# First loads in quarter rows, first products one channel tile at a time, masks first, and longer clock warm-up, in a one-core hybrid decoder block

## The chip, the cores and the metric

The kernel runs on one core of a Trainium2 chip. The metric is the device time of one execution in microseconds (us), from runs without a profiler; the profile is one more execution, taken with the hardware profiler. TensorE is called PE here, VectorE DVE, ScalarE ACT, GpSimd POOL, and SyncE (which issues all the loads) SP.

## What is computed

One layer of a decoder with two groups of heads side by side, for 512 tokens (four tiles of 128) and 1024 channels (eight channel tiles of 128):

```python
h = _rms_norm(x, norm_w[l])
proj = jnp.einsum("btd,dc->btc", h, w_in[l])          # 1024 -> 4096 columns
hq, hf, hi, hg, aq, ak, av, ag = jnp.split(proj, split_points, axis=-1)
o_h = _rms_norm(_hgrn2(hq, hf, hi, lower_bounds[l]), hg_norm_w[l]) * silu(hg)
o_a = _moba(aq, ak, av, q_norm_w[l], k_norm_w[l]) * silu(ag)
x = x + jnp.einsum("btc,cd->btd", concat([o_h, o_a]), w_out[l])
```

Only the start of the first line pair matters here: the transposed, weighted x and its product with the first 512 columns of w_in (`hi`). The row factor of the RMS norm is applied later, when products leave PSUM.

## The kernel before

All is float32. To multiply at near float32 precision, each operand is split into a high part (rounded to the fast matmul format) and a low part (the remainder), and each product is three matmuls: high by high, low by high, high by low. One of these, 128 rows by 512 columns, is called a product below.

**Loads.** SP issues everything in the order of the string `DSEQ`: `x00` is half 0 (512 channels) of token tile 0, 256 KB; `w0` is a weight tile, 256 rows by 512 columns, 512 KB, that is two channel tiles; `nw` is the norm weight, `v` the small vectors. A weight tile lands in `raw`; `split_hi` (ACT, line 109) casts it to `whi`, `split_lo` (DVE, line 117; for weight tile 3 POOL) makes `wlo`.

**Start of PE.** The string `SEQ` is the order by hand of everything up to the end of the first group of columns. Its words, with the functions they call:

- `y7`: `warm_up`, 7 matmuls of 128 by 128 on a tile of ones, whose result nobody reads. The profile has two records for each.
- `nt`: `nw_col`, the norm weight turned into a column (`nwc`).
- `t` a kp: `x_turn`, four transposes: token tiles 2a and 2a+1, channel tiles 2kp and 2kp+1; ACT then copies them out as `hTh` in two instructions 256 wide (line 258). `l` a kp: `x_lo`, DVE makes `hTl` in two instructions (line 266).
- `wh`, `wl` n: the split of weight tile n.
- `p` u kp: `part_hi`, four products of token tile u with weight tile kp (high x with high w, low x with high w, for two channel tiles); `q` u kp: `part_lo`, two products with the low weights.
- `sq` i: ACT squares and sums token tile i; `rs`: the RMS factors (DVE, then POOL); `cv`, `rr`, `cm`: constants, the row of factors, and memory clearing.

The four token tiles' sums stay in four PSUM tiles (`accs`). So before the first product PE transposes all four token tiles for channel tiles 0 to 3 (`t00 t01 t10 t11`, 16 transposes), and then works `p00 q00 p10 q10 p30 q30 p20 q20 ...`. After this string come `p` and `q` of weight tile 3, then seven more groups of columns, the two mixers and the output projection, in an order that a small planner (`drive`) writes down at build time from estimated latencies. The constant masks (`const_tri`) are written at the start of that, in `fill_a`, and the scheduler puts their DVE instructions wherever DVE has room.

Each load has one of eight semaphores in turn, so that the ninth load waits on SP until the first has landed.

Of the kernel before, what the change touches and what calls it, by code (L numbers as in the profile page):

```python
# [8 lines left out]
F32 = mybir.dt.float32  # L9
F32R = mybir.dt.float32r  # L10
I32 = mybir.dt.int32
AF = mybir.ActivationFunctionType
ALU = mybir.AluOpType
# [8 lines left out]
def kernel(  # L22
# [12 lines left out]
    nc = tc.nc  # L35
    P = 128
# [9 lines left out]
    xv = x[0].rearrange("(i p) c -> p i c", p=P)  # L46
# [3 lines left out]
    big = ctx.enter_context(tc.tile_pool(name="big", bufs=1))  # L50
    wpool = ctx.enter_context(tc.tile_pool(name="wpool", bufs=WB))
# [3 lines left out]
    ptr = ctx.enter_context(tc.tile_pool(name="ptr", bufs=2, space=bass.MemoryType.PSUM))  # L55
# [6 lines left out]
    xt = []  # L62
# [5 lines left out]
    def load_x(i, halves=(0, 1)):  # L68
        for hf in halves:
            cs = slice(hf * 512, hf * 512 + 512)  # L70
            nc.sync.dma_start(out=xt[i][:, cs], in_=xv[:, i, cs])  # L71

    def load_vec():
        nc.sync.dma_start(out=vec[0:4, :], in_=lb_logits.rearrange("o (h d) -> (o h) d", d=P))
        nc.sync.dma_start(out=vec[4:5, :], in_=hg_norm_w)
        for r in range(2):
            nc.sync.dma_start(out=vec[5:6, r * DH:(r + 1) * DH], in_=q_norm_w)
            nc.sync.dma_start(out=vec[6:7, r * DH:(r + 1) * DH], in_=k_norm_w)
# [3 lines left out]
    stream = [(w_in[0], c0, kp) for c0 in order for kp in range(KT // 2)]  # L82
# [3 lines left out]
    W = {}  # L86
    raws = {}
    raw0 = []

    def load(n):  # L90
# [11 lines left out]
            in_=src[kp * 256:(kp + 1) * 256, c0:c0 + 512].rearrange("(k p) c -> p k c", p=P))  # L102
        raws[n] = raw

    def split_hi(n):
        raw = raws.pop(n)
        hi = wpool.tile([P, 2, 512], F32R, tag="whi", name="whi")
        lo = wpool.tile([P, 2, 512], F32R, tag="wlo", name="wlo")
        nc.scalar.copy(hi, raw)  # L109
        W[n] = (hi, lo)  # L110
        W["raw", n] = raw
# [13 lines left out]

    POOL_LO = (3,)
    LAT = dict(lm=4.544, lev0=9.2567, lev=4.4882, copy=1.9908, rms=5.7036, silu=15.1764, qk=14.2881, soft=2.5598, softn=0.0041, acopy=4.5215, st=1.5748, ch=6.6909, DEPTH=2)
    SEQ = 'y7 nt t00 wh0 t01 sq0 t10 l00 t11 wl0 p00 q00 l01 wh1 p10 q10 l10 p30 q30 wl1 t03 l11 p20 q20 t12 t02 sq1 p01 q01 wh2 l03 l12 sq3 wh3 p21 q21 p11 q11 sq2 l02 p31 q31 wl2 p32 q32 rs wl3 p02 q02 p22 q22 cv t13 p12 q12 rr cm l13'
    DSEQ = 'x00 nw x10 w0 x20 x30 x01 x31 x11 w1 x21 w2 w4 v w3 w5'
    POOL_LO = (3,)  # L130
    for w in DSEQ.split():
        if w == "nw":
            nc.sync.dma_start(out=vec[32:40, :], in_=norm_w.rearrange("o (k p) -> (o k) p", p=P))  # L133
        elif w == "v":
            load_vec()
        elif w[0] == "x":
            load_x(int(w[1]), (int(w[2]),))
        else:
            load(int(w[1]))
    for n in range(WB, WB + RB):  # L140
# [31 lines left out]
    def mm(o, a, b, start, stop, us):  # L172
        nc.tensor.matmul(o, a, b, start=start, stop=stop)  # L173
        clock[0] += us

    def tr(o, a):
        nc.tensor.transpose(o, a, ident)  # L177
        clock[0] += 0.109
# [82 lines left out]
    def x_lo(a, kp):  # L261
        tp = X["tp", a, kp]
        for d in range(2):
            kt = 2 * kp + d
            ts_ = slice(a * 256, a * 256 + 256)
            nc.vector.scalar_tensor_tensor(hTl[:, kt, ts_], tp[:, d * 256:d * 256 + 256], nwc[:, kt:kt + 1],
                                           hTh[:, kt, ts_].bitcast(F32), op0=ALU.mult, op1=ALU.subtract)


    def acc_tile(wide):  # L270
        return (psc if wide else pacc).tile([P, 512], F32, tag="sc" if wide else "acc", name="acc")
# [465 lines left out]
    def const_tri():  # L737
        prow = const.tile([P, 1], I32, name="prow")
        nc.gpsimd.iota(prow, pattern=[[0, 1]], base=0, channel_multiplier=1)
        ccol = const.tile([P, 32], I32, name="ccol")  # L740
        nc.gpsimd.iota(ccol, pattern=[[1, 32]], base=0, channel_multiplier=0)
        s32 = const.tile([P, 1], I32, name="s32")
        nc.vector.tensor_single_scalar(s32, prow, 31, op=ALU.bitwise_and)
        sb = s32.to_broadcast([P, 32])
        xr = const.tile([P, 32], I32, name="xr")
        nc.vector.tensor_tensor(xr, ccol, sb, op=ALU.bitwise_xor)
        gt = const.tile([P, 32], I32, name="gt")
        nc.vector.tensor_tensor(gt, ccol, sb, op=ALU.is_gt)
        dd = const.tile([P, 32], I32, name="dd")
        nc.vector.tensor_tensor(dd, xr, gt, op=ALU.mult)  # L750
        nc.vector.tensor_single_scalar(eqf, xr, 0, op=ALU.is_equal)
        nc.vector.tensor_single_scalar(lmask[:, 0, :], dd, 1, op=ALU.is_ge)
        for n, l in enumerate((2, 4)):
            bit = 1 << (l - 1)
            nc.vector.tensor_single_scalar(lmask[:, 3 * n + 1, :], dd, bit, op=ALU.is_ge)
            sbit = const.tile([P, 1], I32, name=f"sbit{l}")
            nc.vector.tensor_single_scalar(sbit, prow, bit, op=ALU.bitwise_and)
            for z in range(2):
                side = const.tile([P, 1], I32, name=f"side{l}{z}")
                nc.vector.tensor_single_scalar(side, sbit, z * bit, op=ALU.is_equal)  # L760
                part = const.tile([P, 32], I32, name=f"part{l}{z}")
                nc.vector.tensor_tensor(part, dd, side.to_broadcast([P, 32]), op=ALU.mult)
                nc.vector.tensor_single_scalar(lmask[:, 3 * n + 2 + z, :], part, 2 * bit, op=ALU.is_ge)
# [35 lines left out]


    def fill_a():
        const_tri()
        yield from group(1, True, ev_f)
        yield from group(2, True, ev_silu_t(q2[:, 0]))
        yield from group(3, False, ev_silu(G))
        yield from group(4, True, ev_silu_t(gT))
        const_dist()
        yield from group(5, False, ev_qk("K", ("f", "k", "i", "KL"), kgs))
        yield from group(6, False, ev_qk("Q", ("q",), qgs))
        yield from group(7, False, ev_v)  # L810

    with tc.manual_schedule(engines={mybir.EngineType.PE}):
        with tc.manual_schedule():
            accs = {}

            def part(u, kp, low):
                us = slice(u * P, (u + 1) * P)
                if u not in accs:
                    accs[u] = acc_tile(u >= 2)
                hi, lo = W[kp]  # L820
                for d in range(2):
                    kt = 2 * kp + d
                    wh, wl = hi[:, d, :], lo[:, d, :]
                    prods = ((hTh[:, kt, us], wl),) if low else ((hTh[:, kt, us], wh), (hTl[:, kt, us], wh))
                    for j, (a, b) in enumerate(prods):
                        mm(accs[u], a, b, kt == 0 and not low and j == 0, kt == KT - 1 and low, 0.216)

            def part_hi(u, kp):
                part(u, kp, False)

            def part_lo(u, kp):
                part(u, kp, True)

            acts = dict(cm=const_masks, cv=const_vec, sq=x_sq, rs=x_rstd, rr=x_rows, y=warm_up, nt=nw_col, t=x_turn, l=x_lo, p=part_hi, q=part_lo,
                        wh=split_hi, wl=split_lo)
            for w in SEQ.split():
                name = w.rstrip("0123456789")
                acts[name](*([int(w[1:])] if name == "y" else [int(ch) for ch in w[len(name):]]))
            for n in range(4, WB):
                split(n)  # L840
            for u in range(4):
                part_hi(u, 3)
                part_lo(u, 3)
                ev_i(u, accs[u])
            for kp in range(4):
                del W[kp]
                split(kp + WB)

        q2 = big.tile([P, 2, HH, T], F32, tag="q", name="q2")
        q = q2[:, 1]  # L850
        G = big.tile([P, NT, 512], F32, tag="G", name="G")
        gT = big.tile([P, NP, T], F32, tag="gT", name="gT")
        spawn(levels(0))
        spawn(levels(1))
        spawn(states())
        spawn(chunks())
        fa = fill_a()
        started = [False]

        def filler():  # L860
            yield from fa
            start_attention()
            wait_for(*[("read", n) for n in range(NT)])
            yield from out_h()

        drive(filler())
        for _ in out_a():
            pass
# [27 lines left out]
```

## Time and profile before

| | us |
|---|---|
| median of 3 runs (lowest, highest) | 295.99 (295.94, 296.63) |
| the profiled execution | 297.17 |
| its span, first to last instruction | 295.4 |
| PE busy in the span | 287.6 (97%) |
| DVE, ACT, POOL busy | 175.0, 132.7, 57.1 |

The profiled execution took 1.18 us more than the median of the runs. PE is busy nearly throughout; the exception that concerns the change is the first 11 us. A matmul's record covers more than its share of the pipeline, so what a matmul costs is read from the distance between the starts of two that follow each other.

### The profile page before, as it was taken

What the parts mean: (1) busy time and instruction counts of PE and PEld (TensorE: products, weight loads), DVE (VectorE), ACT (ScalarE), POOL (GpSimd) and SP (SyncE); (2) the same over time, 40 slices, a digit from 0 to 9 for tenths busy, and PEclk for the clock granted to TensorE, in tenths of its full rate; (3) what the DMA queues carried; (4) which work ended last, traced back from release to release, by engine and by line L of the source; (5) the groups of instructions that cost most, each with busy time, mean ns of one, the idle gap of its engine ahead of it and who ended that gap; (6) DMA issues with size and microseconds to landing.
All of it is one profiled execution on the core that took longest, in us unless ns stands there. A gap on an engine that the chain in (4) does not pass through costs nothing.

```text
span 295.4 us, 5115 instructions
## 1 busy us (share of the span) xinstructions
PE 287.6 (97%) x1945; PEld 236.7 (80%) x1945; DVE 175.0 (59%) x379; ACT 132.7 (45%) x248; POOL 57.1 (19%) x92
## 2 busy tenths in 40 slices
PE   7799999999999999999999999999999999999995
PEld 6588888888787777898888888888887787878884
DVE  3552653653699998357855785585384585653232
ACT  3754644420430475225511743753577676763000
POOL 1004201064000000010274223320004534330000
PEclk9999999999999999999999999999999999999999
DMA  6972375160260006100620099468287000000123
GB/s 189 352 282 104 15 106 201 43 242 0 73 213 4 2 2 227 60 0 0 215 73 0 8 261 208 95 168 207 47 229 279 0 2 0 2 2 2 71 101 112
DMA packets 21546, 31.00 MB, mean 105 GB/s; under 512 B 1413, under 2 KB 8338, under 8 KB 21522
## 3 DMA queue, kind: packets, MB, share of 16 engines
q1 hardware_dynamic: 21522, 30.68, 35.5%
q8 instruction: 15, 0.25, 0.3%
q14 instruction: 9, 0.07, 0.1%
HBM read 25.17 MB, written 2.10 MB: 92 GB/s over the span
## 4 chain that ended last, share of the span: by engine, by line
PE 93%; DMA 5%; SPq 1%; DVE 0%; issue 0%; DVEq 0%
PE acc L173 74%; PE tp L177 6%; PE ot L173 4%; PE sc L173 3%; PE pl L173 3%; DMA res<-in_x_dram 3%; DMA x<-in_x_dram 2%; PE ops L173 2%; PE us L173 1%; SPq L71 0%; DVE res L681 0%; SPq L100 0%; DVE res L717 0%; SPq L133 0%; PE tpv L778 0%
## 5 line engine op out<-in xcount | busy, mean ns | idle before, releaser
L173 PE MATMUL acc<-whi,hTh 128*128 128x512 f32 x160 | 65.3, 408 | 0.0
L173 PE MATMUL acc<-whi,hTl 128*128 128x512 f32 x160 | 63.0, 394 | 0.0
L173 PE MATMUL acc<-wlo,hTh 128*128 128x512 f32 x160 | 60.0, 391 | 0.0
L117 DVE TENSOR_TENSOR wlo<-raw,whi 128x1024 fp32r<-128x1024 f32 x39 | 47.1, 1230 | 12.1 <-ACT whi L109 11.6
L109 ACT CAST whi<-raw 128x1024 fp32r<-128x1024 f32 x40 | 41.5, 1048 | 13.4 <-DMA raw<-in_w_in_dram 6.3
L173 PE MATMUL acc<-hTh,whi 128*128 128x512 f32 x96 | 38.2, 397 | 0.0
L173 PE MATMUL acc<-hTh,wlo 128*128 128x512 f32 x96 | 37.5, 391 | 0.0
L173 PE MATMUL acc<-hTl,whi 128*128 128x512 f32 x96 | 37.4, 389 | 0.0
L163 POOL TENSOR_TENSOR r<-v,mh 128x8 f32<-128x8 f32 (+1 forms) x12 | 17.2, 1430 | 99.6 <-DVE v L161 99.5
L173 PEld LDWEIGHTS acc<-whi,hTl 128*128 128x128 f32 x160 | 30.3, 190 | 6.4
L173 PEld LDWEIGHTS acc<-whi,hTh 128*128 128x128 f32 x160 | 30.3, 190 | 6.3
L173 PEld LDWEIGHTS acc<-wlo,hTh 128*128 128x128 f32 x160 | 30.4, 190 | 5.9
L615 POOL TENSOR_SCALAR scr<-scr,rl 128x512 f32<-128x512 f32 (+3 forms) x32 | 17.0, 536 | 47.2 <-DVE rl L614 38.5
L173 PEld LDWEIGHTS acc<-hTh,wlo 128*128 128x128 f32 x96 | 18.0, 188 | 4.0 <-DVE wlo L117 0.2
L173 PEld LDWEIGHTS acc<-hTh,whi 128*128 128x128 f32 x96 | 18.0, 188 | 3.6
L173 PEld LDWEIGHTS acc<-hTl,whi 128*128 128x128 f32 x96 | 18.1, 188 | 3.5
L612 ACT ACTIVATE scr<-scr,nm 128x512 f32<-128x512 f32 (+3 forms) x32 | 17.7, 556 | 6.7 <-DVE nm L608 6.4
L173 PE MATMUL acc<-whi,mTa 128*128 128x512 f32 (+1 forms) x72 | 20.4, 367 | 0.0
L681 DVE TENSOR_TENSOR res<-acc,res 128x512 f32<-128x512 f32 x15 | 10.3, 689 | 15.7 <-PE acc L173 13.3
L177 PE MATMUL tp<-ident,scr 128*128 128x128 f32 x128 | 19.1, 275 | 0.0
L608 DVE CUSTOM_DVE_ANT_0 scr<-sc,bias 128x512 f32<-128x512 f32 (+3 forms) x32 | 14.6, 487 | 6.5 <-PE sc L173 6.2
L177 PEld LDWEIGHTS tp<-ident,scr 128*128 128x128 f32 x128 | 15.0, 140 | 4.0 <-issue 1.4
(138 smaller groups left out, 428.4 us busy)
## 6 DMA issues: line engine op xcount, KB each, us to landing
raw<-in_w_in_dram SPq DMA_DIRECT2D x32, 512.0 KB, 3.7
raw<-in_w_out_dram SPq DMA_DIRECT2D x8, 512.0 KB, 3.9
x<-in_x_dram SPq DMA_DIRECT2D x8, 256.0 KB, 6.4
res<-in_x_dram SPq DMA_DIRECT2D x2, 1024.0 KB, 9.1
out_dram<-res SPq DMA_DIRECT2D x7, 256.0 KB, 2.0
K<-K SPq DMA_DIRECT2D x8, 128.0 KB, 5.9
KL<-KL SPq DMA_DIRECT2D x8, 128.0 KB, 5.9
Q<-scr SPq DMA_DIRECT2D x8, 128.0 KB, 3.7
```

The source lines that it names most:

```text
L109: nc.scalar.copy(hi, raw)
L117: eng.tensor_sub(lo, raw, hi.bitcast(F32))
L163: nc.gpsimd.tensor_tensor(r, v, mh[:, 0:n], op=ALU.pow)
L173: nc.tensor.matmul(o, a, b, start=start, stop=stop)
L177: nc.tensor.transpose(o, a, ident)
L608: nc.vector.tensor_tensor_reduce(out=z[:, 0:n], in0=sc[:, 0:n], in1=bias[:, j, T - n:T], op0=ALU.add, op1=ALU.min, scale=1.0, scalar=3e38, ...
L612: nc.scalar.activation(z[:, 0:n], z[:, 0:n], AF.Exp, bias=nm, scale=-1.0, accum_out=l)
L615: nc.gpsimd.tensor_scalar(z[:, 0:n], z[:, 0:n], rl, 1.0, op0=ALU.mult, op1=ALU.mult)
L681: nc.vector.tensor_tensor(res[hf][:, u, :], ps, res[hf][:, u, :], op=ALU.add)
```

## The change

The new words are: `X` i qr, a quarter row (256 channels, 128 KB) of token tile i; `W` d, 128 rows (256 KB) of weight tile 0; `ct`, the masks, now first; `s` i kp, two transposes for one token tile (`x_turn1`), with copies 128 wide; `k` i kp, the low part of the same; `A0`, `B0`, the high part of the two halves of weight tile 0 (ACT); `a0`, `b0`, their low parts (DVE); `H` u kt and `L` u kt, the two high products and the one low product of token tile u with a single channel tile.

```diff
-    SEQ = 'y7 nt t00 wh0 t01 sq0 t10 l00 t11 wl0 p00 q00 l01 wh1 p10 q10 l10 p30 q30 wl1 t03 l11 p20 q20 t12 t02 sq1 p01 q01 wh2 l03 l12 sq3 wh3 p21 q21 p11 q11 sq2 l02 p31 q31 wl2 p32 q32 rs wl3 p02 q02 p22 q22 cv t13 p12 q12 rr cm l13'
-    DSEQ = 'x00 nw x10 w0 x20 x30 x01 x31 x11 w1 x21 w2 w4 v w3 w5'
+    SEQ = ('ct y10 nt s00 y14 A0 k00 a0 B0 H00 s10 L00 y2 H01 b0 k10 L01 H10 L10 t10 H11 L11 l10 wh1 t01 p20 q20 l01 wl1 '
+           't11 p30 q30 l11 p01 q01 sq0 t03 p11 q11 t12 t02 sq1 p21 q21 wh2 l03 l12 sq3 wh3 p31 q31 sq2 l02 wl2 p32 q32 '
+           'rs wl3 p02 q02 p22 q22 cv t13 p12 q12 rr cm l13')
+    DSEQ = 'X00 nw W0 X10 W1 X20 X30 w1 X01 X11 X21 X31 x01 x11 x31 x21 w2 w3 w4 v w5'
...
+    def load_x_quarter(i, qr):
+        cs = slice(qr * 256, qr * 256 + 256)
+        nc.sync.dma_start(out=xt[i][:, cs], in_=xv[:, i, cs])
...
+        nc.sync.dma_start(out=raws[0][:, d], in_=src[rows, c0:c0 + 512])
+
+    def half_hi(d):
...
+        nc.scalar.copy(W[0][0][:, d], raws[0][:, d])
+
+    def half_lo(d):
+        hi, lo = W[0]
+        nc.vector.tensor_sub(lo[:, d], raws[0][:, d], hi[:, d].bitcast(F32))
...
+    def x_turn1(i, kp):
...
+            tr(tp[:, d * P:(d + 1) * P], xt[i][:, kt * P:(kt + 1) * P])
...
     def fill_a():
-        const_tri()
...
+            def step1(u, kt, low):
...
+                prods = ((hTh[:, kt, us], wl),) if low else ((hTh[:, kt, us], wh), (hTl[:, kt, us], wh))
```

The number of products and of transposes is the same; warm-up matmuls go from 7 to 26 (10, 14 and 2). From the planner on, the order on PE and POOL is the same as before.

The first place is PE's queue from its start to the first products. `wp` is the warm-up result, `tpn` the norm weight, `tp` a transposed piece of x, `acc` a sum; x_79 holds token tiles 0 and 1, x_80 token tiles 2 and 3; the brackets name what the instruction waits for. Before:

```order
L241 MATMUL wp<-scr 128x128 x6
L245 MATMUL tpn<-ident,vec 128x8 [waits DMAHW1_49,Pool_49]
L177 MATMUL tp<-ident,x_79 128x128 [waits DMAHW0_49]
L177 MATMUL tp<-ident,x_79 128x128 [waits DMAHW2_49]
L177 MATMUL tp<-ident,x_79 128x128 x6
L177 MATMUL tp<-ident,x_80 128x128 [waits DMAHW4_49,DVE_49]
L177 MATMUL tp<-ident,x_80 128x128 [waits DMAHW5_49]
L177 MATMUL tp<-ident,x_80 128x128 x2
L177 MATMUL tp<-ident,x_80 128x128 [waits DVE_49,PE_49]
L177 MATMUL tp<-ident,x_80 128x128 x3
L173 MATMUL acc<-whi,hTh 128x512 [waits Activation_49]
```

The same place in the changed kernel:

```order
L268 MATMUL wp<-scr 128x128 x9
L272 MATMUL tpn<-ident,vec 128x8 [waits DMAHW1_49,Pool_49]
L204 MATMUL tp<-ident,x_79 128x128 [waits DMAHW0_49]
L204 MATMUL tp<-ident,x_79 128x128
L268 MATMUL wp<-scr 128x128 x14
L200 MATMUL acc<-whi,hTh 128x512 [waits PE_49,Activation_49]
L200 MATMUL acc<-whi,hTl 128x512 [waits DVE_49]
L204 MATMUL tp<-ident,x_79 128x128 [waits DMAHW3_49]
L204 MATMUL tp<-ident,x_79 128x128
L200 MATMUL acc<-wlo,hTh 128x512 [waits DVE_49]
L268 MATMUL wp<-scr 128x128 [waits PE_49]
L200 MATMUL acc<-whi,hTh 128x512 [waits Activation_49]
```

Two transposes now stand ahead of the first product instead of 16; fourteen warm-up matmuls stand between those two and the first product.

The second place is ACT's queue from the copies of `t03` on. `hTh` copies come in pairs, `sq` is a square, and `whi<-raw_94` (before) or `whi<-raw_99` (changed) are weight tiles 2 and 3. Before:

```order
L258 ACTIVATE hTh<-tp,nwc 128x256 [waits PE_49]
L258 ACTIVATE hTh<-tp,nwc 128x256
L223 ACTIVATE sq,ssx<-x_79 128x1024 [waits DMAHW2_49,DMAHW0_49]
L109 CAST whi<-raw_94 128x1024 [waits DMAHW3_49]
L223 ACTIVATE sq,ssx<-x_80 128x1024 [waits DMAHW7_49,DMAHW5_49,Activation_49]
L109 CAST whi<-raw_94 128x1024 [waits DMAHW3_49]
L223 ACTIVATE sq,ssx<-x_80 128x1024 [waits DMAHW4_49,DMAHW2_49,Activation_49]
```

Changed:

```order
L250 ACTIVATE sq,ssx<-x_79 128x1024 [waits DMAHW4_49,DMAHW0_49]
L285 ACTIVATE hTh<-tp,nwc 128x256 [waits PE_49]
L285 ACTIVATE hTh<-tp,nwc 128x256
L285 ACTIVATE hTh<-tp,nwc 128x256 [waits PE_49]
L285 ACTIVATE hTh<-tp,nwc 128x256
L285 ACTIVATE hTh<-tp,nwc 128x256 [waits PE_49]
L285 ACTIVATE hTh<-tp,nwc 128x256
L250 ACTIVATE sq,ssx<-x_79 128x1024 [waits DMAHW5_49,DMAHW3_49,DMAHW1_49]
L130 CAST whi<-raw_99 128x1024 [waits DMAHW0_49]
L250 ACTIVATE sq,ssx<-x_80 128x1024 [waits DMAHW6_49,DMAHW3_49,Activation_49]
```

ACT's order from the copies of `t12` and `t02` to the cast of weight tile 2 is the same in both. What moved stands on PE: of the 24 products with weight tile 1, all came after `t12 t02` before, and now 12 come ahead of those transposes (`p01 q01 p11 q11`) and 12 behind them, and then follows the first product with weight tile 2.

## Rows read from the trace of the kernel before

**Rows 1.** The page, part 1: busy us, share of the span, instructions

```profile
PE 287.6 (97%) x1945; PEld 236.7 (80%) x1945; DVE 175.0 (59%) x379; ACT 132.7 (45%) x248; POOL 57.1 (19%) x92
```

**Rows 2.** The timeline of PE, first 15 us (start, length, instruction, count, idle)

```profile
1.04 3.36 PE L241 MATMUL wp<-scr 128*128 128x128 f32 x14 [1.04 <-DVE warm L151]
4.33 0.27 PE L245 MATMUL tpn<-ident,vec 8*128 8x8 f32 x1
4.53 0.47 PE L177 MATMUL tp<-ident,x 128*128 128x128 f32 x1
5.63 1.76 PE L177 MATMUL tp<-ident,x 128*128 128x128 f32 x7 [0.63 <-DMA x<-in_x_dram]
8.96 0.45 PE L177 MATMUL tp<-ident,x 128*128 128x128 f32 x1 [1.57 <-DMA x<-in_x_dram]
9.96 1.75 PE L177 MATMUL tp<-ident,x 128*128 128x128 f32 x7 [0.55 <-DMA x<-in_x_dram]
11.36 0.77 PE L173 MATMUL acc<-whi,hTh 128*128 128x512 f32 x1
...
12.36 0.63 PE L173 MATMUL acc<-whi,hTh 128*128 128x512 f32 x1
...
13.21 0.80 PE L173 MATMUL acc<-wlo,hTh 128*128 128x512 f32 x2
13.85 0.40 PE L173 MATMUL acc<-whi,hTh 128*128 128x512 f32 x1
```

**Rows 3.** The waits of the first 15 us (waiter, releaser, us, times, longest)

```profile
PE tp L177 <- DMA x<-in_x_dram: 2.8, 3, 1.6
```

**Rows 4.** Busy time by stage, 10 to 15 us; the 1.00 is the granted clock

```profile
10.00:15.00 5.00, 5.00 (x18) 4.28 (x19) 2.47 (x6) 3.66 (x7) 0.00 (x0) 1.00 1.03 391
```

**Rows 5.** PE's timeline later: records of 128 by 128 matmuls at the fast rate

```profile
130.02 0.38 PE L173 MATMUL ops<-it,AT 128*128 128x128 f32 x2
...
131.58 0.39 PE L173 MATMUL ops<-scr,q 128*128 128x128 f32 x2
```

**Rows 6.** PE's timeline around eight transposes

```profile
17.97 0.62 PE L173 MATMUL acc<-wlo,hTh 128*128 128x512 f32 x2
18.43 1.03 PE L177 MATMUL tp<-ident,x 128*128 128x128 f32 x8
19.22 0.47 PE L173 MATMUL acc<-whi,hTh 128*128 128x512 f32 x1
19.53 0.39 PE L173 MATMUL acc<-whi,hTl 128*128 128x512 f32 x1
```

**Rows 7.** The timeline of ACT and DVE behind these transposes

```profile
19.06 1.57 ACT L258 ACTIVATE hTh<-tp,nwc 128x256 fp32r<-128x256 f32 x4 [0.98 <-PE tp L177]
...
19.94 1.66 DVE L266 SCALAR_TENSOR_TENSOR hTl<-tp,nwc,hTh 128x256 fp32r<-128x256 f32 x4 [0.94 <-ACT hTh L258]
...
20.51 1.07 ACT L223 ACTIVATE sq<-x 128x1024 f32<-128x1024 f32 x1
...
21.55 1.06 ACT L109 CAST whi<-raw 128x1024 fp32r<-128x1024 f32 x1
...
22.64 1.23 DVE L117 TENSOR_TENSOR wlo<-raw,whi 128x1024 fp32r<-128x1024 f32 x1 [1.05 <-ACT whi L109]
```

**Rows 8.** PE's timeline, first product with weight tile 2, and the one after six

```profile
24.79 0.39 PE L173 MATMUL acc<-whi,hTh 128*128 128x512 f32 x1
...
26.15 0.39 PE L173 MATMUL acc<-whi,hTh 128*128 128x512 f32 x1
```

**Rows 9.** The timeline: what loads held up, ACT

```profile
8.03 1.04 ACT L109 CAST whi<-raw 128x1024 fp32r<-128x1024 f32 x1 [0.62 <-DMA raw<-in_w_in_dram]
...
10.79 1.06 ACT L223 ACTIVATE sq<-x 128x1024 f32<-128x1024 f32 x1 [0.97 <-DMA x<-in_x_dram]
```

**Rows 10.** The timeline: POOL, and PE's first product with wlo of weight tile 3

```profile
27.00 2.38 POOL L117 TENSOR_TENSOR wlo<-raw,whi 128x1024 fp32r<-128x1024 f32 x1
...
32.03 0.62 PE L173 MATMUL acc<-wlo,hTh 128*128 128x512 f32 x2
```

More of the change, by code (lines that the diff above doesn't have):

```diff
@@ L103, in load, with load_half @@
         raws[n] = raw
+    def load_half(d):
+        src, c0, kp = stream[0]
+        if d == 0:
+            raw0.append(big.tile([P, 2, 2, 512], F32, tag="f", name="raw0"))
+            raws[0] = raw0[0][:, 0]
+        rows = slice(kp * 256 + d * P, kp * 256 + d * P + P)
+        nc.sync.dma_start(out=raws[0][:, d], in_=src[rows, c0:c0 + 512])
+    def half_hi(d):
+        if d == 0:
+            W[0] = tuple(wpool.tile([P, 2, 512], F32R, tag=t, name=t) for t in ("whi", "wlo"))
+        nc.scalar.copy(W[0][0][:, d], raws[0][:, d])
+    def half_lo(d):
+        hi, lo = W[0]
+        nc.vector.tensor_sub(lo[:, d], raws[0][:, d], hi[:, d].bitcast(F32))
     def split_hi(n):
@@ L137 @@
             load_x(int(w[1]), (int(w[2]),))
+        elif w[0] == "X":
+            load_x_quarter(int(w[1]), int(w[2]))
+        elif w[0] == "W":
+            load_half(int(w[1]))
         else:
@@ L266, in x_lo, with x_lo1 @@
             nc.vector.scalar_tensor_tensor(hTl[:, kt, ts_], tp[:, d * 256:d * 256 + 256], nwc[:, kt:kt + 1],
+                                           hTh[:, kt, ts_].bitcast(F32), op0=ALU.mult, op1=ALU.subtract)
+    def x_turn1(i, kp):
+        tp = ptr.tile([P, 512], F32, tag="tr", name="tp")
+        X["tp1", i, kp] = tp
+        for d in range(2):
+            kt = 2 * kp + d
+            tr(tp[:, d * P:(d + 1) * P], xt[i][:, kt * P:(kt + 1) * P])
+        for d in range(2):
+            kt = 2 * kp + d
+            nc.scalar.activation(hTh[:, kt, i * P:(i + 1) * P], tp[:, d * P:(d + 1) * P],
+                                 AF.Copy, scale=nwc[:, kt:kt + 1])
+    def x_lo1(i, kp):
+        tp = X["tp1", i, kp]
+        for d in range(2):
+            kt = 2 * kp + d
+            ts_ = slice(i * P, (i + 1) * P)
+            nc.vector.scalar_tensor_tensor(hTl[:, kt, ts_], tp[:, d * P:(d + 1) * P], nwc[:, kt:kt + 1],
                                            hTh[:, kt, ts_].bitcast(F32), op0=ALU.mult, op1=ALU.subtract)
@@ L826, in part, with step_hi, step_lo @@
                         mm(accs[u], a, b, kt == 0 and not low and j == 0, kt == KT - 1 and low, 0.216)
+            def step1(u, kt, low):
+                us = slice(u * P, (u + 1) * P)
+                if u not in accs:
+                    accs[u] = acc_tile(u >= 2)
+                hi, lo = W[kt // 2]
+                wh, wl = hi[:, kt % 2, :], lo[:, kt % 2, :]
+                prods = ((hTh[:, kt, us], wl),) if low else ((hTh[:, kt, us], wh), (hTl[:, kt, us], wh))
+                for j, (a, b) in enumerate(prods):
+                    mm(accs[u], a, b, kt == 0 and not low and j == 0, False, 0.216)
+            def step_hi(u, kt):
+                step1(u, kt, False)
+            def step_lo(u, kt):
+                step1(u, kt, True)
             def part_hi(u, kp):
@@ L834 @@
             acts = dict(cm=const_masks, cv=const_vec, sq=x_sq, rs=x_rstd, rr=x_rows, y=warm_up, nt=nw_col, t=x_turn, l=x_lo, p=part_hi, q=part_lo,
-                        wh=split_hi, wl=split_lo)
+                        wh=split_hi, wl=split_lo, ct=const_tri, s=x_turn1, k=x_lo1, H=step_hi, L=step_lo,
+                        A=half_hi, B=lambda _: half_hi(1), a=half_lo, b=lambda _: half_lo(1))
             for w in SEQ.split():
```

## The prediction

> **What bounds the kernel now.** I read the page first. PE is busy 97% of the span [rows 1], the order on PE after the first group of columns is the same before and after, and the change touches only the first 26 us. So the question is one number: how much sooner, or later, PE reaches a given product early on. I take the end of the six products `p32 q32` (token tile 3, weight tile 2), from where both kernels do the same work in the same order. Before, that point is 26.15 us [rows 8].
>
> Then PE's timeline of the start [rows 2]. PE warms up from 1.04 to 4.33 us (14 records, 0.235 us apart), then transposes when loads allow. The waits say it was x that was late, 2.8 us in all [rows 3]. The first product starts at 11.36 us, and the first ones are slow: 12.36 to 13.21 is 0.425 us each, while later products are 0.227 us apart [rows 2, 8]. 512 columns at 1.2 GHz are 0.427 us, at 2.4 GHz 0.213 us, so TensorE's clock rose between 13.21 and 13.85 us, near 13.6. The row by stage says granted clock 1.00 all through [rows 4], so that column doesn't show this step; the distances between starts do. Before the rise PE had worked without a gap since 9.96 us, that is 3.65 us. The stretch from 1.04 to 5.0 us was followed by a gap, and the transposes from 5.63 us are still 0.25 us apart: no rise there [rows 2].
>
> **The change part by part.** From the first product to 26.15 us, before takes 14.79 us. It holds 54 products (24 with weight tile 0, 24 with weight tile 1, six with weight tile 2), 54 x 0.229 = 12.37 us; four transposes and then eight, 0.44 and 0.87 us (the eight: records start at 17.97 two by two, so the next product was due at 18.43; by the pair at 19.22 and 19.53 it counts as 19.30) [rows 6]; the rest, 1.1 us, is the slow clock.
>
> *When the first product starts now.* Warm-ups at the low clock cost 0.235 us a record, at the high clock 0.111 (the 128 by 128 matmuls from 130.02 to 131.58, 14 records) [rows 2, 5]. PE starts at 1.04 us and nothing interrupts it: `y10` lasts longer than the loads of `nw` and `X00` need, since at 4.33 and 4.53 us both were there before [rows 2]. I take the same delay to the rise as the trace shows once, 3.65 us: 4.7 us. By then 15.5 of the 20 records are done; the other 4.5 take 0.5, the norm weight and two transposes 0.35, and the 28 records of `y14` 3.1 us. The first product can start at 8.65 us. Is its data there? `hTl` for one tile is two copies and two subtractions, no dearer than the 256-wide ones: after the transposes at 5.5 us, 0.65 to the start of ACT, 0.8 and 0.9 [rows 7], 7.9 us. The first half of weight tile 0: the whole tile, behind two halves of x, was there at 8.03 us [rows 9]; the half stands behind one quarter, and even at 8.0 its cast of about 0.53 us (half of 1.04) ends at 8.56. So the warm-ups, not data, set the start. Gain 11.36 - 8.65 = 2.7 us.
>
> *The slow products* go, since the warm-ups take the slow time: 1.1 us gained.
>
> *Transposes behind the first product.* Of the 16 that stood ahead of it, 14 now come after it: 14 x 0.11 = 1.5 us lost [rows 6]. The two warm-ups `y2` cost four records, 0.44 us.
>
> *A short wait at `p20`.* The four transposes of `t10` come just ahead: by the pattern of the eight, ACT starts 0.64 us after the transposes, takes 0.8 for a pair, and DVE's first `hTl` is there 1.95 us after the start [rows 6, 7]. PE has 0.44 + 0.69 + 0.44 + 0.23 = 1.8 us of work until it needs it. Lost: 0.2 us with the semaphore.
>
> *A new wait at `p32`.* Before, `t12 t02` at 18.43 us were followed by 24 products ahead of `p32`, now by 12. ACT needs after the first of these transposes: the four copies, the square of tile 1, the cast of weight tile 2, whose end is 22.61 us, that is 4.18 us later, and DVE's low part ends at 23.87, 5.44 us later [rows 6, 7]. ACT's order is unchanged. Before, PE came to `p32` at 24.79 us, 6.36 after [rows 8], and waited for nothing. Now it comes after 0.87 + 12 x 0.229 = 3.6 us, waits 0.6 for the cast, does four products in 0.92, and waits 0.3 for the low part. Lost: 0.9 us. This is what is late next.
>
> *Behind that.* POOL's low part of weight tile 3 hangs on the same ACT chain; it ended at 29.38 us, 10.95 after the transposes, and its reader came at 32.03, 13.6 after [rows 10]. The reader now comes 12 products earlier and 0.9 later, 11.75 after: still 0.8 us of cover. If that goes, the rest shows as a wait at the low products of token tile 0.
>
> *Edits at nothing.* More and smaller loads: up to `X11`, 1.83 MB are issued; before, the same bytes (x00, x10, w0, x20, x30, x01) had landed when the square of tile 0 started at 10.79 us [rows 9]. They are needed at 8.65 + 3.9 = 12.5 us, so 1.7 us of cover; without it PE would wait by the difference. SP issues the new loads behind one another and the ninth waits for the first; `w2` still stands far ahead of its use (21 us). The masks moved first on DVE: some 2.5 us of small instructions in a time in which DVE has only the norm weight's copy to do, due at about 5.2 us; the place they leave was idle DVE time.
>
> **The sum**, against the profiled execution: -2.7 - 1.1 + 1.5 + 0.44 + 0.2 + 0.9 = -0.7 us, give or take 0.1 for rounding. All behind runs on PE in the same order, so the shift stays. The profiled execution took 297.17 us, 1.18 above the median of the runs; I carry the difference over to the median: 295.99 - 0.7 = **295.3 us**. A measurement of this kernel can tell about 0.3% (0.9 us) from no change, so this is just inside "the same". If the clock rises d later in both kernels, after loses 0.53 d (records at 0.235 for 0.111) and before 0.5 d (products at 0.43 for 0.23): the sum hardly moves, and that is why I trust it more than its parts.
>
> **The rivals.**
>
> *The rise differs between executions.* One unbroken stretch of about the same length was followed by no rise and one by a rise, so the trace doesn't fix the moment. If before's products usually run slow for longer than in this execution, as late again is 3.65 us more, 1.8 us lost; half of that is 0.9. With after unchanged the difference is -0.7 - 0.9 = -1.6 us: 294.4. For it: the runs spread by 0.7 us. Against it: two of three are within 0.05. The Trainium skill (TensorE: Matmul & The Clock Gate, Part 1: The HAM clock gate) says that the activity monitor runs free of the kernel's start and that the moment of the rise therefore differs from run to run; the two stretches agree with that, and no run here shows it. Chance 0.27.
>
> *The new wait at `p32` doesn't come*, because ACT does its chain faster than the pattern of one execution: then 0.9 us more is gained, -1.6 us, 294.4. Against it: ACT's durations are steady, and the order is the same. Chance 0.13.
>
> *The warm-ups hold the products back: slower.* `y14` stands between the transposes and the first product whatever the data. The forecast dies where the first product starts later than 8.65 + 0.7 + 0.9 = 10.2 us, that is where the rise comes later than about 7.5 us. If it comes as late again as I took, at 8.3 us, the first product is at 10.5 and the kernel at +1.2 us, 297.2. If matmuls on ones don't raise it at all (14 records of them did not in the trace), the 28 records take 6.6 us, the first product is at 13.0 and the first ones are slow again: 13.0 - 8.65 + 1.1 + 0.5 (`y2`) - 0.7 = +5.3 us, 301.3. Chance 0.06 for each.
>
> *The change doesn't do what it says*: loads in quarters land no sooner, PE waits at `s00` or `H00`. The bounds above leave at most some tenths; it is within the forecast's range.
>
> **How the numbers follow.** Forecast 0.48 (its own range 295.1 to 296.4, with half a microsecond of doubt on the waits upward), the two faster rivals 0.40, the slower ones 0.12. Range 294.1 to 296.6: it takes in both faster cases down to -1.9 us and the late rise in part; it leaves out the warm-ups that raise nothing, the rest of the late rise and a tail below. Faster by over 0.3%: 0.40; within: 0.48; slower: 0.12.
>
> **What would show it.** In the profile after: the first record of a product at 8.5 to 9 us, with starts 0.23 us apart from the first on; warm-up records changing from 0.235 to 0.111 us apart somewhere between 4.5 and 8 us; a gap of 0.6 us on PE before the first product with weight tile 2, ended by ACT, and one of 0.3 ended by DVE four products later; `p32 q32` done at about 25.5 us. Wrong would be: the first product past 10.2 us, slow first products, PE waiting on x or weights, a wait of more than 1 us anywhere before 26 us, or a shift at 26 us that the end doesn't show.

## The result, and the profile after

The changed kernel is slower: a median of 298.06 us (296.75 to 301.20, 22 runs) against 296.85 us (293.63 to 300.04, 22 runs) for the kernel before, 1.2 us more. The ratio, which leaves out unusually slow executions while these medians are of all 22, is 1.0053 with a 95% interval of [1.003, 1.0077]. That is about +1.6 us (0.9 to 2.3) where -0.7 was forecast, and 298.06 us is outside the range. The larger sample also moved before's own median up from the 295.99 us of three runs.

The profiled execution of the changed kernel has a span of 298.3 us and took 301.20 us, the longest of its 22 runs: it holds one event that 20 of them don't show. The first view to read is the mean granted clock, then the stages near 226 us:

```profile
core 0: 298.3 us, clock 0.994
```

```profile
225.00:228.00 3.00, 1.40 (x10) 1.17 (x9) 1.41 (x6) 0.68 (x2) 0.00 (x0) 0.99 0.83 319
228.00:231.50 3.50, 3.50 (x10) 2.76 (x9) 1.54 (x9) 1.94 (x9) 2.49 (x5) 0.52 0.02 8
```

The column behind POOL's is the granted clock. In the second stage it is 0.52, the lower of the two levels, 1.2 GHz. PE's timeline there shows what came ahead of it:

```profile
227.34 0.50 PE L200 MATMUL acc<-whi,mThh 128*128 128x512 f32 x1 [1.60 <-DVE res L727]
...
228.73 0.63 PE L200 MATMUL acc<-wlo,mThh 128*128 128x512 f32 x1
229.16 0.63 PE L200 MATMUL acc<-whi,mThl 128*128 128x512 f32 x1
...
231.79 0.38 PE L204 MATMUL tp<-ident,scr 128*128 128x128 f32 x2
```

PE idled 1.6 us, waiting for DVE, and DVE for the load of x for the residual (`res`); after that the clock fell, and matmuls 512 wide stood 0.43 us apart until 231.3 us. The same instructions in the profile of before:

```profile
226.11 0.50 PE L173 MATMUL acc<-whi,mThh 128*128 128x512 f32 x1 [0.70 <-DVE res L681]
...
228.97 0.60 PE L177 MATMUL tp<-ident,scr 128*128 128x128 f32 x4
```

Against these the changed kernel pays +0.9 us for the longer wait and +1.6 us for the slow matmuls. Only 2 of its 22 runs have a mean clock this low (0.994, spans of 298.2 and 298.3 us); the other 20 have 0.998 to 1.0 and spans of 294.8 to 296.8 us. So this event is most of the 2.9 us between the two profiled spans, and not the cause of the difference between the medians.

Part of that difference lies outside the span altogether. A run's time is longer than its span, in the kernel before by 1.72 to 1.83 us in each of the 76 runs made beside the experiments below. In the changed kernel it is longer by 1.73 to 2.90 us, 2.21 on average, about 0.4 us more than in before. Of the variants below, those that keep `y14` show it too (2.0 to 2.1 us on average) and those with `y6` in its place don't (1.8). No trace shows what happens there, and the cause stays open.

What the change does stands in PE's timeline of the start. It answers to [rows 2, 8]:

```profile
1.04 4.64 PE L268 MATMUL wp<-scr 128*128 128x128 f32 x20 [1.04 <-DVE warm L178]
5.61 0.27 PE L272 MATMUL tpn<-ident,vec 8*128 8x8 f32 x1
5.81 0.54 PE L204 MATMUL tp<-ident,x 128*128 128x128 f32 x2
6.19 3.29 PE L268 MATMUL wp<-scr 128*128 128x128 f32 x28
9.23 0.48 PE L200 MATMUL acc<-whi,hTh 128*128 128x512 f32 x1
9.55 0.39 PE L200 MATMUL acc<-whi,hTl 128*128 128x512 f32 x1
...
13.54 0.48 PE L200 MATMUL acc<-whi,hTh 128*128 128x512 f32 x1
14.10 0.50 PE L200 MATMUL acc<-whi,hTl 128*128 128x512 f32 x1
14.44 0.39 PE L200 MATMUL acc<-whi,hTh 128*128 128x512 f32 x1
...
23.55 0.61 PE L200 MATMUL acc<-wlo,hTh 128*128 128x512 f32 x2
24.61 0.50 PE L200 MATMUL acc<-whi,hTh 128*128 128x512 f32 x1 [0.45 <-ACT whi L130]
24.95 0.39 PE L200 MATMUL acc<-whi,hTl 128*128 128x512 f32 x1
...
25.42 0.39 PE L200 MATMUL acc<-whi,hTl 128*128 128x512 f32 x1
25.87 0.73 PE L200 MATMUL acc<-wlo,hTh 128*128 128x512 f32 x2
26.44 0.39 PE L200 MATMUL acc<-whi,hTh 128*128 128x512 f32 x1
```

There is no gap up to the first product, there are no slow products, and PE waits for no load. The first product comes at 9.23 us. The three waits are where the prediction put them: at `p20` (steps of 0.56 and 0.34 us where 0.31 and 0.23 were due, about 0.35 us), at `p32` (24.61 where 24.01 was due, and one late step more, 0.7 us, ended by ACT's cast) and at `q32` (0.33 us). What ended those at `p20` and `q32` shows in the waits of PE's weight loads (PEld): DVE's low parts of x (`hTl`) and of the weights (`wlo`).

```profile
PEld acc L200 <- DVE wlo L138: 0.5, 1, 0.5
PEld acc L200 <- DVE hTl L293: 0.4, 1, 0.4
```

The point that was 26.15 us before is 26.44: +0.3 us, not -0.7. The rest of the way to 217 us keeps that +0.3 us. So against this one profile of before the start explains 0.3 us, and not 1.6.

### The profile page after: what moved, and what is told of

It is laid out like the page before. It is cut to its first block, busy times and chain, and to the rows that moved or that the text cites. A ratio compares the mean times of both kernels' runs of the same rounds, so it can differ in the third digit from the quotient of the medians.

```text
span 298.3 us, 5203 instructions
## 1 busy us (share of the span) xinstructions
PE 291.6 (98%) x1983; PEld 240.3 (81%) x1983; DVE 177.8 (60%) x382; ACT 133.0 (45%) x251; POOL 57.2 (19%) x92
## 4 chain that ended last, share of the span: by engine, by line
PE 87%; DMA 9%; SPq 1%; ACT 1%; DVE 1%; issue 0%; DVEq 0%
PE acc L200 70%; PE tp L204 5%; PE ot L200 3%; DMA raw<-in_w_in_dram 3%; DMA res<-in_x_dram 3%; PE sc L200 3%; PE pl L200 3%; DMA x<-in_x_dram 2%; PE ops L200 2%; PE us L200 1%; SPq L75 1%; SPq L104 0%; DVE wlo L138 0%; ACT sq L250 0%; ACT whi L130 0%; SPq L115 0%
## 5 line engine op out<-in xcount | busy, mean ns | idle before, releaser
L138 DVE TENSOR_TENSOR wlo<-raw,whi 128x1024 fp32r<-128x1024 f32 x38 | 45.9, 1229 | 10.6 <-ACT whi L130 10.2
L130 ACT CAST whi<-raw 128x1024 fp32r<-128x1024 f32 x39 | 40.5, 1048 | 16.2 <-DMA raw<-in_w_in_dram 8.6
L200 PEld LDWEIGHTS acc<-whi,hTh 128*128 128x128 f32 x160 | 30.1, 188 | 6.9 <-ACT whi L130 0.9
L200 PEld LDWEIGHTS acc<-whi,hTl 128*128 128x128 f32 x160 | 30.1, 188 | 6.6 <-DVE hTl L293 0.4
L654 DVE CUSTOM_DVE_ANT_0 scr<-sc,bias 128x512 f32<-128x512 f32 (+3 forms) x32 | 14.6, 487 | 6.5 <-PE sc L200 6.2
```

The costliest lines, as they stand in the source:

```text
L138: eng.tensor_sub(lo, raw, hi.bitcast(F32))
L654: nc.vector.tensor_tensor_reduce(out=z[:, 0:n], in0=sc[:, 0:n], in1=bias[:, j, T - n:T], op0=ALU.add, op1=ALU.min, scale=1.0, scalar=3e38, ...
```

## The experiments

Two theories stood at first. The start theory: the loss lies in the first 37 us. The late theory: it lies at the residual's load, where the profile shows the most. As a landmark on PE for the start I use the transpose of the RMS factors (`rp<-ident,rst`), one instruction in both kernels, behind everything that the change touches; it is at 30.99 us in the profile of before and at 31.31 in that of the change.

**The wait at `p32` taken away.** This and the next three variants ran on one chip, beside 35 runs of the kernel before.

```diff
-           't11 p30 q30 l11 p01 q01 sq0 t03 p11 q11 t12 t02 sq1 p21 q21 wh2 l03 l12 sq3 wh3 p31 q31 sq2 l02 wl2 p32 q32 '
+           't11 p30 q30 l11 sq0 t03 t12 t02 sq1 p01 q01 p11 q11 wh2 l03 l12 sq3 wh3 p21 q21 p31 q31 sq2 l02 wl2 p32 q32 '
```

> The changed kernel with one edit: the transposes t12 t02 stand ahead of the 12 products p01 q01 p11 q11 again, as they did before the change. Start theory (the loss lies in the first 37 us, at the new wait for weight tile 2): PE's wait of 0.7 us at p32 and of 0.25 us at q32 go, the first product of the second group of columns comes 0.9 us sooner than in the changed kernel at the same moment of the clock's rise, and the ratio to before falls from 1.005 to 1.002 or less. Late theory (the loss lies near 226 us, at the load of x for the residual): the start gains the 0.9 us as well, but the time stays within 0.1% of the changed kernel's, 1.005, because the later wait eats it.

Measured: ratio to before 1.0017, interval [0.999, 1.0043]. PE's timeline around the same place, with the landmark:

```profile
23.34 0.62 PE L200 MATMUL acc<-wlo,hTh 128*128 128x512 f32 x2
23.80 0.39 PE L200 MATMUL acc<-whi,hTh 128*128 128x512 f32 x1
...
24.48 0.39 PE L200 MATMUL acc<-whi,hTl 128*128 128x512 f32 x1
24.70 0.62 PE L200 MATMUL acc<-wlo,hTh 128*128 128x512 f32 x2
...
30.01 0.27 PE L259 MATMUL rp<-ident,rst 128*4 128x128 f32 x1
```

No late step is left at `p32` and `q32`, and the landmark comes 1.3 us sooner: 0.95 for the wait and 0.33 because the first product came at 8.90 us in this execution. The ratio is the start theory's number (1.002 or less). Its interval overlaps that of the changed kernel, so by its time alone this variant doesn't settle the question.

**Fewer warm-ups ahead of the first product.**

```diff
-    SEQ = ('ct y10 nt s00 y14 A0 k00 a0 B0 H00 ...
+    SEQ = ('ct y10 nt s00 y6 A0 k00 a0 B0 H00 ...
```

> The changed kernel with 6 instead of 14 warm-up matmuls in the second batch. Start theory: if the second batch holds the products back, the first product comes at 8.0 us instead of 9.2 (its low half of x is there at about 7.4 us and its weights at 7.6), and the kernel gains 0.9 us where the clock has risen by then; if the clock then rises later, the first products run at half speed and it gains nothing or loses up to 1 us. Late theory: within 0.2% of the changed kernel.

Measured: ratio 1.0015 [0.9984, 1.0045].

```profile
5.17 0.44 PE L204 MATMUL tp<-ident,x 128*128 128x128 f32 x2
5.45 1.50 PE L268 MATMUL wp<-scr 128*128 128x128 f32 x12
6.83 0.50 PE L200 MATMUL acc<-whi,hTh 128*128 128x512 f32 x1
...
28.98 0.27 PE L259 MATMUL rp<-ident,rst 128*4 128x128 f32 x1
```

The first product started at 6.83 us, 2.4 us sooner than in the changed kernel and sooner than the 8.0 I expected, so its data was there by then in this execution. Of the 2.4 us, 0.6 come from a clock that rose earlier (the two transposes start at 5.17 instead of 5.81 us, behind the same instructions); the other 1.8 are the eight warm-ups less, 16 records 0.11 us apart. So `y14` held the products back for nothing, as the slower rival of the prediction said. The landmark is 2.3 us sooner, but the ratio falls by 0.0038 only, about 1.1 us; where the rest goes isn't shown. By its threshold (a first product later than 10.2 us) a start at 9.23 should still have been a gain; what that threshold missed is told below.

**The residual's load in quarters.** In both kernels:

```diff
-            nc.sync.dma_start(out=res[hf], in_=xv[:, :, cs])
+            for uu in range(NT):
+                nc.sync.dma_start(out=res[hf][:, uu, :], in_=xv[:, uu, cs])
```

In the kernel before:

> The kernel before with one edit: each of the two 1 MB loads of x for the residual (near 217 us) is cut into four of 256 KB, so that its first user waits for a quarter. Late theory: PE's wait of 0.7 us near 226 us goes, and the executions in which the clock falls there are fewer: 0.5 to 1.5 us faster than before. Start theory says nothing of it: at most the 0.7 us.

In the changed kernel:

> The changed kernel with the same cut of the residual loads. Late theory: the wait of 1.6 us and the fall of the clock behind it go, and the time comes within 0.1% of the kernel before with that cut. Start theory: it stays 1.2 to 1.6 us (0.4 to 0.5%) above the kernel before with that cut.

Measured: before with the cut, 1.0040 [1.0004, 1.0075] of before; the change with the cut, 1.0098 [1.0061, 1.0135]. The cut helps neither, and the distance between the two, 0.58%, is that of the uncut pair (0.53%), where the late theory asked for less than 0.1%. With the 20 of 22 runs that have no such low mean clock and are longer than before's all the same (a median span of 295.7 us, against 294.5 in the 76 runs of before), that speaks against the late theory. The test is not a clean one, since PE's wait near 226 us was not taken away but changed its cause, as the waits of PE in the first of the two show:

```profile
PE tp L177 <- POOL scr L615: 1.7, 1, 1.7
PE tp L177 <- DMA x<-in_x_dram: 1.1, 2, 0.8
```

PE no longer waits for `res`; it now waits 1.7 us for POOL's scaling of the softmax (0.8 us in the changed kernel with the cut). The second line was the surprise that led on: this kernel, whose start is that of before, waited 1.1 us for x, not 2.8 [rows 3].

**The kernel before, unchanged, three times more.**

> The kernel before, unchanged, for a second profile of it. If the moment at which TensorE's clock rises differs between executions, this one may rise during the first warm-up matmuls (near 4 to 5 us); then the first products are 0.23 us apart from the first on, the point that was 26.15 us comes 1 us or more sooner, and the span is 294 to 294.7 us. If it rises at 13.6 us again, the span is near 295.4 again.

> The kernel before, unchanged, for a third profile. Theory of the late loads (the profile that the prediction rests on met x late, 2.8 us of waiting; usually it is about 1.1 us, as in the second profile): the first product at 9.5 to 10.2 us, and the transpose of the RMS factors, a landmark on PE that is at 30.99 us there and at 31.31 in the changed kernel, at 29 to 30.1 us. If the first product is past 11 us again, the second profile was the exception.

> The same once more, a fourth profile of the kernel before: the first product at 9.5 to 10.2 us and the landmark at 29 to 30.1 us by the theory of the late loads; past 11 us and near 31 us otherwise.

PE's timeline of the second profile:

```profile
5.39 1.76 PE L177 MATMUL tp<-ident,x 128*128 128x128 f32 x7 [0.39 <-DMA x<-in_x_dram]
7.46 0.45 PE L177 MATMUL tp<-ident,x 128*128 128x128 f32 x1 [0.31 <-DMA x<-in_x_dram]
8.27 1.76 PE L177 MATMUL tp<-ident,x 128*128 128x128 f32 x7 [0.37 <-DMA x<-in_x_dram]
9.68 0.78 PE L173 MATMUL acc<-whi,hTh 128*128 128x512 f32 x1
10.25 0.63 PE L173 MATMUL acc<-whi,hTl 128*128 128x512 f32 x1
...
12.35 0.39 PE L173 MATMUL acc<-whi,hTh 128*128 128x512 f32 x1
...
29.51 0.27 PE L232 MATMUL rp<-ident,rst 128*4 128x128 f32 x1
```

of the third:

```profile
10.53 0.78 PE L173 MATMUL acc<-whi,hTh 128*128 128x512 f32 x1
...
29.96 0.27 PE L232 MATMUL rp<-ident,rst 128*4 128x128 f32 x1
```

and of the fourth:

```profile
9.30 0.78 PE L173 MATMUL acc<-whi,hTh 128*128 128x512 f32 x1
...
13.29 0.57 PE L173 MATMUL acc<-whi,hTl 128*128 128x512 f32 x1
...
29.91 0.27 PE L232 MATMUL rp<-ident,rst 128*4 128x128 f32 x1
```

Compare the gaps with those of [rows 2]: x was waited for 1.1 us in the second, 1.8 in the third, 0.6 in the fourth. The first product is at 9.68, 10.53 and 9.30 us, and the landmark at 29.51, 29.96 and 29.91, on average 29.8 us. One of the three is past the bound of 10.2 that I gave, none is past 11. The profile behind the prediction, with 11.36 and 30.99, was the one in which x came latest. With it and with the kernel of the cut residual loads, which has the same start (9.80 and 30.04 us), the mean of five profiles is 10.1 us for the first product and 30.1 us for the landmark.

The first products are slow in all five (0.43 us apart until 12.3 to 13.7 us), so nothing here supports the other guess, that the profiled execution was unlucky in its clock. It isn't ruled out for every execution: 35 of the 76 runs of before beside these experiments have a mean clock of 0.994 or less, and none of the five profiles is one of them.

Against 29.8 us the changed kernel's landmark at 31.31 (31.44 in the two other profiles with its order in the first 30 us) is +1.5 us, against the mean of five it is +1.2. The three executions took 295.76, 296.05 and 296.32 us, all less than the median of 296.85, so 29.8 us may be early for the runs that the result compares.

**Half rows again.**

```diff
-    DSEQ = 'X00 nw W0 X10 W1 X20 X30 w1 X01 X11 X21 X31 x01 x11 x31 x21 w2 w3 w4 v w5'
+    DSEQ = 'x00 nw W0 x10 W1 x20 x30 w1 x01 x11 x31 x21 w2 w3 w4 v w5'
```

> The changed kernel with x loaded in half rows again (x00 nw W0 x10 W1 x20 x30 w1 x01 x11 x31 x21 ...), weight tile 0 still in two pieces. If quarter rows are worth nothing, since the second warm-up holds the first product to 9.2 us anyway: within 0.2% of the changed kernel (1.0053). If they are what brings the first product forward: it comes later than 9.2 us, ended by a load, and the kernel is 0.3% or more slower than the changed one.

Measured: 1.0067 [1.0044, 1.009], with the first product at 9.34 us and the landmark at 31.44. That is the changed kernel's time within 0.14%: behind `y14` the quarter rows are worth nothing that these runs can show.

**Both repairs of the changed kernel.** `y6` for `y14`, and the order of the first experiment.

> The changed kernel with both edits: t12 t02 ahead of the products p01 q01 p11 q11, and 6 instead of 14 warm-up matmuls in the second batch. If the loss is the sum of the wait at p32 (0.9 us) and of the products held back by the warm-up (about 1 us on average, 2.4 us where the clock rises early): 1.9 us faster than the changed kernel, ratio to before 0.998 to 0.999, and spans near 293.5 to 294.5 us where the clock doesn't fall later. If either gain is eaten by a later wait: 1.001 or more.

Measured: 0.9994 [0.9968, 1.002]; first product at 7.40 us, landmark at 28.59. It undoes the whole loss (1.7 us against the changed kernel's ratio, and the two intervals don't overlap), a little less than the 1.9 expected. But a landmark 1.2 us ahead of the three profiles of before brings less than that in time. PE gives it back at the residual's load:

```profile
224.75 0.50 PE L200 MATMUL acc<-whi,mThh 128*128 128x512 f32 x1 [1.79 <-DVE res L727]
```

In the second profile of before the same product started at 224.72 us, after a wait of 0.82. SP issued the load at 214.77 us here and at 215.72 there, and its first user started at 224.0 us in both: issued 0.95 us sooner, the load was no sooner there. Why stays open.

**More warm-up alone, in before.** The fourth part of the change, longer warm-up, without the others and in another place, where PE waits for x:

```diff
-    SEQ = 'y7 nt t00 wh0 t01 sq0 t10 l00 t11 ...
+    SEQ = 'y7 nt t00 wh0 t01 sq0 y4 t10 l00 t11 ...
```

> The kernel before with four more warm-up matmuls between the transposes of channel tiles 2 and 3 of token tiles 0 and 1 and those of token tiles 2 and 3, where PE waits for x. Slow-products theory (the first products of before usually run at 1.2 GHz, as in its profile): it gains up to 1.1 us, ratio 0.997. Mode theory (in most executions of before the clock has risen by the first product, and the profiled one was an unlucky one): it gains 0.4 us at most, ratio 0.9985 to 1.001, and the longest spans without a later fall of the clock (295 to 296 us) get rare.

> The kernel before with four warm-up matmuls ahead of the transposes of token tiles 2 and 3 once more, on another occasion. If its gain was real: ratio to before 0.991 to 0.998. If it was luck with the later falls of the clock: 0.998 to 1.002.

Measured: 0.9935 [0.9906, 0.9965] and, on another chip, 0.9917 [0.9887, 0.9947]. PE's timeline of the second run:

```profile
5.51 0.99 PE L177 MATMUL tp<-ident,x 128*128 128x128 f32 x7 [0.51 <-DMA x<-in_x_dram]
6.34 1.06 PE L241 MATMUL wp<-scr 128*128 128x128 f32 x8
7.58 0.30 PE L177 MATMUL tp<-ident,x 128*128 128x128 f32 x1 [0.19 <-DMA x<-in_x_dram]
8.13 0.98 PE L177 MATMUL tp<-ident,x 128*128 128x128 f32 x7 [0.25 <-DMA x<-in_x_dram]
8.87 0.48 PE L173 MATMUL acc<-whi,hTh 128*128 128x512 f32 x1
9.18 0.40 PE L173 MATMUL acc<-whi,hTl 128*128 128x512 f32 x1
...
27.52 0.27 PE L232 MATMUL rp<-ident,rst 128*4 128x128 f32 x1
```

The seven transposes from 5.51 us are already fast (0.99 us, where the profile of before has 1.76). They stand ahead of the new warm-ups and behind the same instructions as in before, so in this execution the clock rose early without them. What the four do here is to fill the wait for x that follows; they cost no time of their own, since PE still waits for x on either side, and the products are fast from the first on. In the profile of the first run the clock rose later: the seven transposes took 1.75 us, the four warm-ups (eight records) 1.7, PE had no wait for x left behind them, and the first product came at 10.41 us, but it and those behind it were fast too; the landmark is at 28.99. Both medians are ahead of both kernels, by 1.2 us against before in the first run (294.89 against 296.07) and 2.5 in the second (294.14 against 296.60), at least the 1.1 us that I put on the slow products.

Three more warm-ups at the very front instead, `y10` for `y7`:

> The kernel before with three more warm-up matmuls at the very front (10 instead of 7), as in the changed kernel, and none in the gaps. They end at 5.7 us at the low clock and cover the first wait for x alone; the gaps from 7 to 9 us stay. If what matters is that PE works without a gap up to the products: no gain, 0.999 to 1.002, and the first products are still 0.43 us apart in some executions. If an early rise is enough: 0.996 to 0.998.

Measured: 0.9939 [0.9914, 0.9964], better than either expectation. Its one profile doesn't show how:

```profile
5.76 1.09 PE L177 MATMUL tp<-ident,x 128*128 128x128 f32 x8
8.50 0.30 PE L177 MATMUL tp<-ident,x 128*128 128x128 f32 x1 [1.64 <-DMA x<-in_x_dram]
...
10.92 0.78 PE L173 MATMUL acc<-whi,hTh 128*128 128x512 f32 x1
```

The transposes from 5.76 us were fast, PE then idled 1.6 us for x, the clock fell (granted 0.58 from 8.5 to 12.0 us), and the first products, from 10.92 us, were 0.43 us apart again. Three of its 12 runs have the mean clock of this one, 0.994, and all three a span of 294.6 us; eight have 0.998 to 1.0 and spans of 291.9 to 293.4. So in most executions the early rise seems to last to the products, but no trace of such a run was seen.

## Why the prediction was wrong

Step by step, in the prediction's own terms:

- *The first product's time, "11.36 - 8.65 = 2.7 us" gained.* This failed, on both ends. The 11.36 us was one execution with late loads; four others with the same start show 9.30 to 10.53, on average 9.8, so 1.5 us of the gain wasn't there in them. This is the largest error, and it wasn't in the mechanism but in taking the start of one profiled execution for the kernel's. The row that could have warned was there: 2.8 us of waiting for DMA is a number that can differ from run to run, and the text priced nothing for it to be less. And after came at 9.23, not 8.65, because the clock rose near 6 us and not at 4.7.
- *The slow products, 1.1 us gained:* right. They are slow in all five profiles with before's start and fast in the changed kernel. If anything the term was small: from the first product to the point that was 26.15 us the five take 14.6 to 15.8 us, where 14.79 - 1.1 = 13.7 are due without slow products. That is 0.9 to 2.1 us, 1.4 on average.
- *Transposes and `y2` behind the first product, 1.5 + 0.44 lost:* as priced, as far as the sum can tell: with these terms it comes to 26.2 us, where 26.44 was measured.
- *The waits at `p20`, `p32`, `q32`, 0.2 + 0.6 + 0.3:* the places and the releasers were right, the sizes somewhat low: 0.35, 0.7 and 0.33. Undoing the order that makes the last two gave back 0.95 us at the landmark. So the rival "the wait doesn't come" is out.
- *"The sum hardly moves if the clock rises d later in both":* no run tests the half about the clock. What it left out is that the loads move before's start alone. After hides them behind its warm-ups, before doesn't, and so the difference of the two is as uncertain as one load.
- *The slower rival* had the right place, `y14` ahead of the first product, and its threshold was wrong: measured from an 11.36 us that wasn't typical, it had to pass 10.2 us; from 9.8 us, by the same terms, it decides 1.5 us sooner, at 8.7, and 9.23 is past that.
- *Edits at nothing:* right as far as tested. Half rows again cost 0.14%, within the noise, and PE waited for none of the new loads. The masks moved first and weight tile 0 in two pieces had no run of their own.
- *The rival of the differing rise:* the moment of the rise does differ between executions (near 6.1 us in the changed kernel, 5.2 with the first edit, 4.4 with the second, for the same first 20 records). The Trainium skill's statement that it isn't tied to the kernel's start (TensorE: Matmul & The Clock Gate, Part 1: The HAM clock gate) agrees with these rows. The rival's conclusion, that before usually stays slow for longer, fits the 1.4 us on average in part; it would make the changed kernel faster, and that is not what came.

The corrected sum, against the three later profiles of before: the first product gains 9.8 - 9.23 = 0.6 us (9.8 is the mean of 9.68, 10.53 and 9.30), the slow products 1.1 as forecast. Against these stand 1.5 + 0.44 for what now comes after the first product and 0.35 + 0.7 + 0.33 = 1.4 for the waits. That is 3.3 lost and 1.7 gained, +1.6 us, where the landmark shows +1.5. With the 2.7 us of the prediction in place of the 0.6 the same sum is -0.5, close to the forecast; so this one term turned a loss into a forecast gain.

That the sum meets the ratio's +1.6 us is in part luck. With the measured 1.4 us for the slow products it is +1.3, and with all five profiles of before +1.0, where the landmark shows +1.2. The medians are 1.2 us apart, and about 0.4 us of the loss lies outside the span, where the sum has no term. What is shown is the sign and the two places: with the order at `p32` and the length of `y14` both undone, the loss is gone (0.9994). And of the 2.8 us between the forecast 295.3 and the measured 298.06, 0.9 are before's own median, 296.85 in place of 295.99.

## What to carry to other kernels

Ahead of a forecast of a start that waits for loads, take more than one profile, or price the wait at both ends: a wait for DMA in one trace is a sample, not a constant. Warm-up matmuls belong where the engine waits anyway: four in a gap gained 0.65 to 0.8%, while fourteen between finished transposes and the first product held it back by 1.8 us more than six. And when products are moved ahead of transposes, count what the engine behind the transposes still has to do before the next weights are ready.

## What the runs showed of the hardware that was not expected

PE's wait for the first loads of x was 0.6 to 2.8 us in four executions of the same kernel, and the first product moved with it by 2.1 us (9.30 to 11.36). A wait of 1.6 us in the middle of the kernel was followed by a fall of the clock that cost another 1.6 us in one execution; a wait of 1.79 us at the same place, in the kernel with both repairs, was followed by none, so its length alone doesn't tell. Behind the same instructions the clock had risen by 5.5 us in one execution (the second run with `y4`) and not before 12.3 us in the five profiles with before's start. The time outside the span was 0.2 to 0.4 us longer on average in the variants with fourteen warm-ups in the second batch than in those with six. And cutting a 1 MB load into four for its first user made the kernel 0.4% slower; in its profile another wait, of 1.7 us, had taken the place of that for the load.
